# A hybrid attention layer on one core: keys loaded into the place of their lo, and fourteen steps of gate sets before them

## The chip, the cores and the metric

The kernel runs on one core of a Trainium2 chip (trn2). The metric is device time in microseconds (us) of one execution of the whole program; lower is better. The granted clock of TensorE is read from the profile; its two levels are 1.2 and 2.4 GHz.

## What is computed

One decoder layer on 1024 tokens of width 1024, all in float32: a SwiGLU feed-forward block, then a mixer, then a second SwiGLU block and a final norm. Each block has an RMS norm whose scale and shift come from a condition vector. Only the mixer matters here:

```python
u = modulate(rmsnorm(h, norm2_w), sh2, sc2)
proj = u @ w_in            # q, six key/value sets, gates, retention q k v g, ga, gb
o_nsa = nsa_attention(...) # compressed, selected and sliding-window branches, 8 heads, 2 key groups
o_ret = retention(...)     # 8 heads, chunks of 128 tokens, a state carried from chunk to chunk
mixed = sigmoid(ga) * (o_nsa @ w_nsa_up) + sigmoid(gb) * (o_ret @ w_ret_up)
h = h + gt2 * (mixed @ w_out)
```

Products keep float32 accuracy on TensorE by splitting each operand into a rounded part ("hi") and the rest ("lo") and taking three products, hi x hi, hi x lo and lo x hi.

## The kernel before

**Engines.** TensorE multiplies; ScalarE makes the hi parts (a copy that rounds), VectorE the lo parts (a subtraction); GpSimd does sums; all loads and stores of this part are issued on SP, one queue, in order. The program is written with generators; `weave(main, fill, n)` takes a step of `main` and after it `n` steps of `fill`. The framework's scheduler then orders the instructions of each engine, and each engine runs its own in that order.

**Gate sets.** The projection is computed in sets by a scheme of seven products for two blocks of 128 columns (`set_t` with `wset` and `seven`). A set loads two raw weight blocks of 512 KB (L327) into two of the three places of the tile `raw` (the pool `W2`, `WM = (3, 3)`: three places of `wp` and three of `raw`). GpSimd forms sums of them (L341 to L344, tile `S`), ScalarE and VectorE split them into `wp` (L334, L335). Each product is 12 matmuls of 128x512 (L281), in the order u0, u0, t2, t3, t4, u1, u1 by the name of its moving operand; the results are added up (L391 to L416). The first two products need only the first raw block, the third needs the sums of both. Eight such sets (0 to 7) make the gates `ga` and `gb`: their results pass a sigmoid (L1461) and are stored to `d_gab` (L1462). One set before them makes the keys, which are stored to `d_k` in memory, and two make the queries (`d_q`).

**Retention.** `ret_core` runs twice, once for four heads each, over eight chunks. A chunk is a chain across the engines: load q and k (L903) into `rqk`, rotate (L910 on VectorE, L912 and L913 on GpSimd), transpose (L918), scores (L928), mask (L930), output and state (L937 to L952), mean (L956 to L959), squares and variance (L961, L964). After every fourth chunk the outputs are scaled (L970, L975), gated (L977, with `rg` loaded at L974), transposed (L979), copied to `rb` (L982) and stored to `d_ret` (L983). Steps of the sets are the fill between the chunks' steps.

**Keys and queries.** After the retention a pool `kv` is opened where the retention's pool was; it holds Kh and Kl, hi and lo of two kinds of keys, 128 x 2 x 1024 each, and Q. `keys` loads four halves from `d_k`, each with two loads (L1027) that put the same data on partitions 0 to 63 and 64 to 127, and splits each (L1029, L1030). The halves pass through `self.stage()`, a place of `raw`. `queries` does the same with Q (L1055 to L1057). Then attention begins; its first score products (L1071 with Kh, L1072 with Kl) read Q and the keys, into the four places of `s`.

The part of `run` that sets the order before the change:

```python
        for _ in range(7):
            next(fill, None)
        kv = pool(c_n, "kv", "right")
        self.Q = {}
        weave(itertools.chain(self.keys(kv), self.queries(0, kv, self.stage)), fill, 3)
        drain(fill)
```

The fill holds 77 steps of sets beside the second retention's own; the compression and the two retentions take 40 of them, so that 7, 18 and 12 are left for these three statements.

Of the kernel before, what the change touches and what calls it, by code (L numbers as in the profile page):

```python
# [33 lines left out]
def drain(*gens):  # L34
    for g in gens:
        for _ in g:
            pass


def weave(main, fill, n):  # L40

    done = 0
    for i, _ in enumerate(main, 1):
        while done < i * n:
            next(fill, None)
            done += 1


def f32(ap):
    return ap.bitcast(F32)  # L50


class Layer:
# [963 lines left out]
    def keys(self, pool):  # L1017
        nc = self.nc
        self.Kh = [pool.tile([P, 2, T], F32R, name="Kh%d" % b) for b in range(2)]
        self.Kl = [pool.tile([P, 2, T], F32R, name="Kl%d" % b) for b in range(2)]  # L1020
        for b in range(2):
            src = self.d_k[b].rearrange("(g d) t -> d g t", g=2)
            for hf in range(2):
                s = slice(hf * H2, (hf + 1) * H2)
                a = self.stage()
                for r in range(2):
                    nc.sync.dma_start(a[64 * r:64 * r + 64], src[:, :, s])  # L1027
                kh, kl = self.Kh[b][:, :, s], self.Kl[b][:, :, s]
                nc.scalar.copy(kh, a)  # L1029
                nc.vector.tensor_sub(kl, a, f32(kh))  # L1030
                yield

    def values(self, pool, stage):
# [262 lines left out]
    def run(self):  # L1296
# [3 lines left out]
        nc = self.nc  # L1300
        self.w_in = self.I["w_in"][0].rearrange("(k p) n -> p k n", p=P)

        def pool(ctx, name, side="left"):
            return ctx.enter_context(tc.tile_pool(name=name, bufs=1, side=side, reuse_waits="tile"))
# [178 lines left out]
        def sets():  # L1483
            yield from self.set_t(self.w_in, 768, 1024, us, sp, to({"a": self.d_k[0], "b": self.d_k[1]}))
            for p in (0, 2):
                yield from self.set_t(self.w_in, p * P, (p + 1) * P, us, sp, to({"a": self.d_q[p], "b": self.d_q[p + 1]}))
            for d in range(KD):
                yield from self.set_t(self.w_in, 3352 + d * P, 4376 + d * P, us, sp, to_gate(d))
# [3 lines left out]
        fill = itertools.chain(more, sets())  # L1492
        with ExitStack() as c1:
            weave(self.compress(self.keep, pool(c1, "cmp", "right")), fill, 4)
        for r in range(2):
            with ExitStack() as c1:
                weave(self.ret_core(r, pool(c1, "ret", "right")), fill, 1)
            drain(more)
        for _ in range(7):
            next(fill, None)  # L1500
        kv = pool(c_n, "kv", "right")
        self.Q = {}
        weave(itertools.chain(self.keys(kv), self.queries(0, kv, self.stage)), fill, 3)
        drain(fill)


# [88 lines left out]
```

## Time and profile before

| | us |
|---|---|
| median of 3 runs (2422.99 to 2425.41) | 2424.69 |
| the profiled execution | 2428.69 |
| its span, first to last instruction | 2427.0 |
| PE busy in the span | 2271.1 (94%) |
| DVE busy (VectorE) | 1811.0 (75%) |
| POOL busy (GpSimd) | 1222.3 (50%) |
| ACT busy (ScalarE) | 1051.5 (43%) |

The mean granted clock of TensorE is 0.969 of full speed. In the rows, PE is a matmul, PEld its weight load, SPq a DMA issue on SP; times are from the start of the span. A row of a timeline gives start, duration, engine, line, operation, out<-in, count, and in brackets the idle time before it and what ended that. TensorE's matmuls overlap a little, so that the time of many is read from start to start.

### The profile page before, as it was taken

To read this page: it belongs to the slowest core of one execution; us is meant where nothing else is said; L and a number is where in the kernel's file an instruction comes from. 1 tells how busy PE (TensorE), PEld (TensorE's weight loads), DVE (VectorE), ACT (ScalarE), POOL (GpSimd) and SP (SyncE) were. 2 spreads that over 40 slices of the span, in tenths; PEclk is the share of its full clock that TensorE was granted. 3 is DMA by queue.
4 is the path that set the end of the run, shared out by engine and by line. 5 is a ranking of instruction groups with operands and counts; after the bars stand their busy time and mean duration, and the time that the engine had idled before them with its cause. 6 is when DMAs were issued, how large, how long until landed. Compare 5 with 4: busy or idle time off the path is not lost. (4 is left out here: it accounts for less than half of the span.)

```text
span 2427.0 us, 32641 instructions
## 1 busy us (share of the span) xinstructions
PE 2271.1 (94%) x11563; PEld 1903.5 (78%) x11563; DVE 1811.0 (75%) x2742; ACT 1051.5 (43%) x1902; POOL 1222.3 (50%) x900
## 2 busy tenths in 40 slices
PE   7799999999987999999869999999889999999997
PEld 5678888878876899887757889877668888887885
DVE  8888888578999844667646888859895555558988
ACT  5332222235764322223336777826532222235675
POOL 3856454544476524454434544645664444436437
PEclk8999999999998999999979999989899999999999
DMA  9135656263204444335343311470312222246301
GB/s 348 57 105 168 205 171 202 87 230 131 87 1 146 121 124 129 120 95 159 98 122 129 96 58 44 160 227 1 104 56 83 87 79 79 83 144 220 98 28 70
DMA packets 248886, 288.31 MB, mean 119 GB/s; under 512 B 14852, under 2 KB 169236, under 8 KB 248724
## 3 DMA queue, kind: packets, MB, share of 16 engines
q1 hardware_dynamic: 248608, 286.19, 37.1%
q8 instruction: 91, 1.49, 0.3%
q14 instruction: 71, 0.58, 0.1%
q10 hardware_dynamic: 116, 0.05, 0.0%
HBM read 216.45 MB, written 69.73 MB: 118 GB/s over the span
## 5 line engine op out<-in xcount | busy, mean ns | idle before, releaser
L281 PE MATMUL po<-u0h,wp 128*128 128x512 f32 x944 | 308.2, 399 | 24.1 <-ACT wp L334 14.6
L758 PE MATMUL po<-wp 128*128 128x512 f32 x1128 | 271.7, 398 | 15.6 <-DVE wp L679 14.7
L281 PE MATMUL po<-u1h,wp 128*128 128x512 f32 x880 | 283.2, 392 | 2.5 <-DVE bias L544 2.2
L758 PEld LDWEIGHTS po<-wp 128*128 128x128 f32 x1128 | 214.6, 192 | 68.4 <-DVE wp L679 22.2
L758 PE MATMUL s<-wp 128*128 128x512 f32 x1056 | 250.8, 394 | 13.9 <-DVE wp L679 13.3
L758 PEld LDWEIGHTS s<-wp 128*128 128x128 f32 x1056 | 199.7, 190 | 60.5 <-DVE wp L679 18.2
L334 ACT CAST wp<-S 128x1024 fp32r<-128x1024 f32 x98 | 103.0, 1051 | 299.8 <-PE po L281 295.7
L281 PEld LDWEIGHTS po<-u0h,wp 128*128 128x128 f32 x944 | 181.7, 192 | 64.4 <-ACT wp L334 15.0
L463 POOL TENSOR_TENSOR t<-t,t 128x512 f32<-128x512 f32 x38 | 56.3, 1482 | 297.9 <-DVE t L407 189.2
L281 PEld LDWEIGHTS po<-u1h,wp 128*128 128x128 f32 x880 | 165.9, 189 | 39.1 <-DVE bias L544 2.6
L281 PE MATMUL po<-u0l,wp 128*128 128x512 f32 x472 | 187.8, 398 | 0.0
L281 PE MATMUL po<-u1l,wp 128*128 128x512 f32 x440 | 172.9, 393 | 2.5 <-DVE u1l L243 2.5
L335 DVE TENSOR_TENSOR wp<-S,wp 128x1024 fp32r<-128x1024 f32 x98 | 158.7, 1620 | 15.3 <-ACT wp L334 15.2
L334 ACT CAST wp<-raw 128x1024 fp32r<-128x1024 f32 x98 | 82.0, 837 | 173.7 <-PE po L281 168.7
L341 POOL TENSOR_TENSOR S<-raw 128x512 f32<-128x512 f32 x49 | 68.4, 1396 | 141.1 <-DMA raw<-w_in 77.9
L281 PE MATMUL po<-t4h,wp 128*128 128x512 f32 x392 | 131.8, 397 | 1.8 <-DVE tn L399 1.1
L281 PE MATMUL po<-t3h,wp 128*128 128x512 f32 x392 | 131.8, 396 | 0.8 <-DVE t L395 0.8
L281 PE MATMUL po<-t2h,wp 128*128 128x512 f32 x392 | 131.3, 395 | 0.3 <-DVE tg L412 0.3
L335 DVE TENSOR_TENSOR wp<-raw,wp 128x1024 fp32r<-128x1024 f32 x98 | 114.9, 1173 | 13.7 <-ACT wp L334 13.5
L395 DVE TENSOR_TENSOR t<-tn,po 128x512 f32<-128x512 f32 x57 | 39.1, 685 | 101.2 <-issue 73.7
L1164 DVE TENSOR_TENSOR pl<-pt,ph 128x512 fp32r<-128x512 f32 (+2 forms) x160 | 96.8, 619 | 15.6 <-ACT ph L1163 15.0
L281 PEld LDWEIGHTS po<-u0l,wp 128*128 128x128 f32 x472 | 91.2, 193 | 18.9
(474 smaller groups left out, 6187.2 us busy)
## 6 DMA issues: line engine op xcount, KB each, us to landing
raw<-ffn_w_in SPq DMA_DIRECT2D x88, 512.0 KB, 4.2
raw<-ada_w SPq DMA_DIRECT2D x56, 512.0 KB, 4.4
raw<-w_in SPq DMA_DIRECT2D x40, 512.0 KB, 4.3
d_g<-t SPq DMA_DIRECT2D x50, 256.0 KB, 2.0
d_h<-hT SPq DMA_DIRECT2D x24, 512.0 KB, 4.7
hT<-d_h SPq DMA_DIRECT2D x48, 256.0 KB, 5.4
d_g<-tg SPq DMA_DIRECT2D x38, 256.0 KB, 2.0
fw<-ada_w SPq DMA_DIRECT2D x8, 1024.0 KB, 11.7
```

The costliest lines, as they stand in the source:

```text
L281: nc.tensor.matmul(ps, a, b, start=k == 0 and q == 0, stop=k == n - 1 and q == 2)
L334: nc.scalar.copy(w[:, 0], t)
L335: nc.vector.tensor_sub(w[:, 1], t, f32(w[:, 0]))
L341: nc.gpsimd.tensor_add(s[:, 0:4], b[:, 0:4], b[:, 4:8])
L395: nc.vector.tensor_add(c, u2, p)
L463: nc.gpsimd.tensor_mul(g, g, t)
L758: nc.tensor.matmul(po[d], l[:, e], r, start=k == 0 and z == 0 and not seeded, stop=k == m - 1 and z == 2, skip_group_check=seeded)
L1164: nc.vector.tensor_sub(lo, pt[:, :n], f32(hi))
```

## The change

Each half of the keys is loaded straight into its place in Kl, seen as float32; ScalarE rounds it from there into Kh, and VectorE subtracts Kh from it in place. The keys use no place of `raw` any more; the queries still do. Before the pool of the keys is opened, 14 steps of the fill are taken in place of 7, that is, two sets, and beside keys and queries 2 a step in place of 3 (12 in place of 18); 11 are left for the last statement. Everything computed is the same. Behind L1026 the line numbers of the changed kernel are lower by one.

```diff
@@ keys
             for hf in range(2):
                 s = slice(hf * H2, (hf + 1) * H2)
-                a = self.stage()
+                kh, kl = self.Kh[b][:, :, s], self.Kl[b][:, :, s]
                 for r in range(2):
-                    nc.sync.dma_start(a[64 * r:64 * r + 64], src[:, :, s])
-                kh, kl = self.Kh[b][:, :, s], self.Kl[b][:, :, s]
-                nc.scalar.copy(kh, a)
-                nc.vector.tensor_sub(kl, a, f32(kh))
+                    nc.sync.dma_start(f32(kl[64 * r:64 * r + 64]), src[:, :, s])
+                nc.scalar.copy(kh, f32(kl))
+                nc.vector.tensor_sub(kl, f32(kl), f32(kh))
                 yield
@@ run
-        for _ in range(7):
+        for _ in range(14):
             next(fill, None)
         kv = pool(c_n, "kv", "right")
         self.Q = {}
-        weave(itertools.chain(self.keys(kv), self.queries(0, kv, self.stage)), fill, 3)
+        weave(itertools.chain(self.keys(kv), self.queries(0, kv, self.stage)), fill, 2)
         drain(fill)
```

How the order moves, at three places. First SP, from the last loads of the retention (L974) on; L983 stores the retention's output, the loads from `d_k` and `d_q` are keys and queries, L327 are weights of a set, and the stores to `d_gab` are gates. Before:

```order
L974 DMA rg<-d_rn 128x256 x2
L983 DMA d_ret<-rb 128x512 x2
L1027 DMA raw<-d_k 64x2x512 x2
L327 DMA raw<-w_in 128x8x128 x2
L1055 DMA raw<-d_q 64x2x512 x4
L327 DMA raw<-w_in 128x8x128 x2
L1462 DMA d_gab<-t_10108 128x512
L327 DMA raw<-w_in 128x8x128
L1462 DMA d_gab<-t_10160 128x512
L327 DMA raw<-w_in 128x8x128
```

And now:

```order
L974 DMA rg<-d_rn 128x256 x2
L1461 DMA d_gab<-t_10248 128x512
L327 DMA raw<-w_in 128x8x128
L983 DMA d_ret<-rb 128x512 x2
L1027 DMA Kl_10003<-d_k 64x2x512 x4
L1027 DMA Kl_10004<-d_k 64x2x512 x4
L1461 DMA d_gab<-t_10294 128x512
L1461 DMA d_gab<-tg 128x512
L1461 DMA d_gab<-tn 128x512
L327 DMA raw<-w_in 128x8x128
```

All eight key loads now stand together behind the retention's last store, where six of them stood earlier; of the six weight loads that stood behind the retention, one stands ahead of its last store and one behind the keys, the other four earlier still. The two weight loads left are those of gate set 7.

Second, TensorE at the end of the retention's last chunk (L937 and L939 make its output, L979 transposes the gated outputs). Before:

```order
L928 MATMUL pi<-qT,kT 128x128 x4
L937 MATMUL po<-state_8761,qT 128x128
L939 MATMUL po<-rv,inn 128x64 x2
L937 MATMUL po<-state_8761,qT 128x128
L939 MATMUL po<-rv,inn 128x64 x2
L979 MATMUL po<-ident,xc 128x128 x8
L281 MATMUL po<-u0h,wp 128x512
L281 MATMUL po<-u0l,wp 128x512
```

And now:

```order
L937 MATMUL po<-state_8761,qT 128x128
L939 MATMUL po<-rv,inn 128x64 x2
L937 MATMUL po<-state_8761,qT 128x128
L939 MATMUL po<-rv,inn 128x64 x2
L281 MATMUL po<-u1h,wp 128x512
L281 MATMUL po<-u1l,wp 128x512
L281 MATMUL po<-u1h,wp 128x512 x2
L281 MATMUL po<-u1l,wp 128x512
```

Between the last chunk's output and the transposes there are now a whole product of set 5 (u1) and three of set 6; the first group of transposes stands ahead of set 6's fourth product (t3), the second behind eight of its twelve matmuls. The eight score products of the first attention tile stand, as before, behind a set's second product, now that of gate set 7 (one of the eight a product earlier).

Third, VectorE some 50 us earlier, between two gate sets (L410 to L416 add up the older set's last products, L335 splits the next set's weights, L910 rotates a chunk of the retention). Before:

```order
L407 TENSOR_TENSOR t_9861<-tg,po 128x512
L335 TENSOR_TENSOR wp<-raw,wp 128x1024
L910 TENSOR_TENSOR rb<-rqk,rcs 128x8x32 x2
L411 TENSOR_TENSOR tn<-tn,po 128x512
L412 TENSOR_TENSOR tg<-tg,po 128x512
```

And now:

```order
L407 TENSOR_TENSOR t_9861<-tg,po 128x512
L335 TENSOR_TENSOR wp<-raw,wp 128x1024
L411 TENSOR_TENSOR tn<-tn,po 128x512
L412 TENSOR_TENSOR tg<-tg,po 128x512
L335 TENSOR_TENSOR wp<-S,wp 128x1024
```

The rotation has moved behind the two additions that free the older set's results (and behind a split and the next addition).

## Rows read from the trace of the kernel before

**Rows 1.** The page's first part: busy time, share of the span, instructions.
```profile
PE 2271.1 (94%) x11563; PEld 1903.5 (78%) x11563; DVE 1811.0 (75%) x2742; ACT 1051.5 (43%) x1902; POOL 1222.3 (50%) x900
```
**Rows 2.** Busy time by stretches: PE, PEld, DVE, ACT, POOL, PEclk, DMA share, GB/s.
```profile
1050.00:1100.00 50.00, 49.57 (x278) 41.05 (x277) 34.71 (x63) 13.84 (x19) 20.48 (x20) 1.00 0.33 101
1100.00:1150.00 50.00, 48.01 (x282) 39.06 (x280) 34.64 (x61) 14.06 (x22) 28.07 (x25) 1.00 0.51 154
...
1200.00:1250.00 50.00, 27.28 (x141) 21.57 (x140) 25.62 (x45) 16.86 (x21) 10.57 (x12) 0.69 0.40 108
```
**Rows 3.** Timeline of PE, from the retention's last chunk to the first scores.
```profile
1209.50 0.46 PE L937 MATMUL po<-state,qT 128*128 128x128 f32 x2 [2.22 <-DVE xc L959]
...
1216.49 1.35 PE L979 MATMUL po<-ident,xc 128*128 128x128 f32 x4 [4.65 <-DVE xc L977]
1219.12 1.37 PE L979 MATMUL po<-ident,xc 128*128 128x128 f32 x4 [1.27 <-DVE xc L977]
1235.07 0.79 PE L281 MATMUL po<-u0h,wp 128*128 128x512 f32 x1 [14.58 <-ACT wp L334]
...
1243.29 0.39 PE L1071 MATMUL s<-Kh,Q 128*128 128x512 f32 x1
...
1244.78 0.40 PE L281 MATMUL po<-t2h,wp 128*128 128x512 f32 x1
```
**Rows 4.** Timeline of PE: the starts of u0 and of t2, two products apart.
```profile
1152.95 0.39 PE L281 MATMUL po<-u0h,wp 128*128 128x512 f32 x1
...
1158.39 0.39 PE L281 MATMUL po<-t2h,wp 128*128 128x512 f32 x1
```
**Rows 5.** Timeline of SP: issues of keys and of weights.
```profile
1136.77 0.59 SPq L1027 DMA_DIRECT2D raw<-d_k  x1
...
1162.23 0.48 SPq L327 DMA_DIRECT2D raw<-w_in  x1
...
1188.37 0.59 SPq L1027 DMA_DIRECT2D raw<-d_k  x1
...
1227.28 1.24 SPq L1027 DMA_DIRECT2D raw<-d_k  x2
1228.61 1.33 SPq L327 DMA_DIRECT2D raw<-w_in  x2
```
**Rows 6.** Timeline of ACT: casts of keys and of weights, and a sigmoid.
```profile
1223.74 2.94 ACT L1029 CAST Kh<-raw 128x1024 fp32r<-128x1024 f32 x3
1232.40 1.04 ACT L1029 CAST Kh<-raw 128x1024 fp32r<-128x1024 f32 x1 [5.73 <-DMA raw<-d_k]
1233.97 1.04 ACT L334 CAST wp<-raw 128x1024 fp32r<-128x1024 f32 x1 [0.53 <-DMA raw<-w_in]
...
1249.48 0.63 ACT L1461 ACTIVATE t<-t 128x512 f32<-128x512 f32 x1
```
**Rows 7.** Timeline of PE: the second product of a wait further up, first and next.
```profile
1175.31 0.47 PE L281 MATMUL po<-u0h,wp 128*128 128x512 f32 x1 [2.18 <-DVE tg L412]
...
1179.73 0.60 PE L918 MATMUL pt<-ident,rqk 128*128 128x128 f32 x4
```
**Rows 8.** Timeline of DVE: a rotation, the keys' lo, the sets' last addition.
```profile
1171.04 2.93 DVE L910 TENSOR_TENSOR rb<-rqk,rcs 128x256 f32<-128x256 f32 x2
...
1226.03 3.50 DVE L1030 TENSOR_TENSOR Kl<-raw,Kh 128x1024 fp32r<-128x1024 f32 x3 [6.28 <-DMA d_ret<-rb]
...
1296.84 0.69 DVE L416 TENSOR_TENSOR tn<-tn,po 128x512 f32<-128x512 f32 x1 [1.44 <-PE po L281]
```
**Rows 9.** Timeline of POOL: the first and the third sum of gate set 5.
```profile
1235.75 1.66 POOL L341 TENSOR_TENSOR S<-raw 128x512 f32<-128x512 f32 x1 [18.17 <-DMA raw<-w_in]
...
1238.61 1.28 POOL L342 TENSOR_TENSOR S<-S,raw 128x512 f32<-128x512 f32 x1
```
**Rows 10.** The view of line L1027, the eight key loads of 256 KB.
```profile
DMA to landing us min/median/max: 3.6/3.9/5.6
```
**Rows 11.** The view of line L327, the weight loads of 512 KB.
```profile
DMA to landing us min/median/max: 3.8/4.2/8.8
```

## The prediction

> **What bounds the kernel now.** I read the page's first part, then the busy time by stretches, then TensorE's timeline in the worst stretch, and from its longest wait back through the queues. TensorE (PE) is busy 94% of the span [rows 1], so only stretches where it stands still can give much. One such lies in the middle: from 1050 to 1150 us it idles 0.4 and 2.0 us per 50, from 1200 to 1250 it is busy 27.3 us and its granted clock averages 0.69 [rows 2]. That is the end of the retention, just before the keys. The timeline names four waits there: 2.22 us (VectorE's centred output), 4.65 and 1.27 (its gated output), 14.58 (ScalarE's cast of the next gate set's weights); together 22.7 [rows 3]. From the first of them until after the last the matmuls run slow: the 24 of gate set 5's first two products take from 1235.07 to 1243.29, 8.2 us [rows 3], where 24 like them take from 1152.95 to 1158.39, 5.44, or 2.72 for a product of 12 [rows 4].
>
> Why were those weights so late? Sets take their raw weights from three `raw` places, and the key halves take the same three. The first key load is issued at 1136.8, the sixth at 1188.4, and no weights are issued between 1162.23 and 1228.61 [rows 5]. The keys cannot leave their places: their hi and lo lie where the retention's tiles lie, so the first cast is at 1223.74 [rows 6]. From about 1190 on, the retention's latency has nothing beside it.
>
> **The change, part by part.** The two edits belong together: loading the keys into Kl takes them off `raw`, and 14 steps in place of 7 lets sets be planned ahead of the keys.
>
> *Taken away.* (1) In the new order nearly eleven products of gate sets 5 and 6 (11 x 2.72 = 30 us) move ahead of the last retention transposes, so the four waits have work in them: **22.7 us**. (2) TensorE does not slow there: 8.2 - 5.4 = 2.8 us on the 24 matmuls, and half of the 2.7 us of the two transpose groups [rows 3], 1.3; together **4.1**. (3) Earlier, matmuls start again at 1175.31 after waiting 2.18 us for VectorE's L412 and run slow, 12 of them until 1179.73: 4.4 in place of 2.7 [rows 7]. L412 stood behind the rotary products L910, which took 2.93 us [rows 8]; in the new order L411 and L412 stand ahead of L910. **3.9 us**; it may also stay. Sum 30.7.
>
> *Moved.* The eight key loads no longer run early. Kl's place overlaps the retention's `rb`, so the first load waits until the second store of d_ret has landed. Call E the end of the last transposes (before: 1219.12 + 1.37 = 1220.5 [rows 3]). VectorE waited for that store until 1226.03 [rows 8], E + 5.5. From there I take the flow of the trace of before: a pair of key loads issued at 1227.28, then two weights loads from 1228.61 [rows 5]; the pair was cast at 1232.40, the first weights at 1233.97 [rows 6], and GpSimd took the second at 1235.75 [rows 9]. So the first half MB lands 5.1 us after its issue, each further one 1.6 to 1.8 later; I take 1.7. The four pairs then land at E + 10.6, 12.3, 14.0 and 15.7. SP issues the eight in 8 x 0.62 = 5.0 us (two in 1.24 [rows 5]), done at E + 10.5; the stores behind them wait for results that come later anyway. Each pair is cast in 1.05 us [rows 6] and subtracted in about 1.2 (three in 3.50 [rows 8]). The same instructions were there before, on the same sizes; that they now read and write one tile I cost at nothing.
>
> Who waits? TensorE has, after E, a third of a product and five whole ones (5.33 x 2.72 = 14.5 us), then the eight score products of the first attention tile, about 1.5 us (1243.29 [rows 3] to the next L281 at 1244.78 [rows 3]), so they could end at E + 16.0. Those on the window keys need all four pairs: 15.7 + 1.05 + 1.2 = 17.9, and end near 18.4.
>
> Behind them stands the third product of gate set 7, which needs sums of both its weight loads. The second of these is now on SP behind the eight key loads and three stores of set 6, the last of which waits for a sigmoid that stands on ScalarE behind the second key cast: 12.3 + 1.05 + 0.63 [rows 6] = 14.0. Issued at 14.4, it lands at 18.6 by the median of 4.2 for half a MB [rows 11], or behind the keys at 17.4; I take 18.6. Then GpSimd's three sums, 4.1 us (1235.75 to 1239.9 [rows 9]), cast and subtraction, 2.3: ready at E + 25.0. So **9.0 us** of new waiting (25.0 - 16.0), of which 2.4 is the keys' and 6.6 the weights'. After it I take the slow start that followed the old wait, **2.8**. And **1.5** for ordinary pace beside the retention, between the 0.4 and 2.0 idle per 50 us of [rows 2]; GpSimd now has set 5's four sums among the retention's rotary work there, which is the likeliest part of it. Together 13.3.
>
> Bounds of the new wait: below, 0, if loads run faster than the queue shows; above, each pair takes as long as a single load's median, 3.9 [rows 10], in place of 1.7: the last pair lands at 22.3, the weights at 26.2, ready 32.6, wait 16.6. I take 9.0, since the rows of three half MBs in a row are the nearest.
>
> *At nothing.* Masks and values for attention need places that set 7 frees; their loads were issued 10 us and more before use and still follow the sums, ahead of 13.6 us of products. If that cover failed it would cost one load, 4 us.
>
> **The sum.** 30.7 - 13.3 = 17.4 us. Against the profiled execution, 2428.69 - 17.4 = 2411.3; that execution lies 4.0 above the median of the runs, so the median goes from 2424.69 to **2407.3**. About 0.2% (5 us) is what the measurement can tell from no change.
>
> The Trainium skill speaks against this change: "Trainium Kernel Development and Optimization", section Best Practices, asks to overlap loads with compute by double buffering, and here an early load is made late. The trace of before shows the overlapped load being the one that does the harm [rows 5]; by the rule alone the sum would be only the 9 us added, and its case is the last rival.
>
> **The rivals.**
> - *All hidden* (0.12): the loads are done before TensorE comes to them, and no slow start follows. 30.7 - 1.5 = 29.2 gained, 2395.5. Against it: SP's new order, in which the weights stand behind the keys.
> - *The wait mostly moves* (0.18): pairs land 3.9 apart, wait 16.6. 30.7 - 16.6 - 2.8 - 1.5 = 9.8 gained, 2414.9; without term (3), 5.9 and 2418.8. For it: a single key load of a quarter MB does take 3.9 to land [rows 10]. Against: the three half MBs in [rows 5, 6, 9].
> - *No change to speak of* (0.06): the same, with the order of the first attention tiles, which also shifts, costing a few us.
> - *Slower* (0.04): the exposed keys become the bound. If each of the eight loads waited for the one before (8 x 3.9), the last would land at E + 36.7, the weights at 40.9, ready at 47.2: wait 31.2, and 30.7 - 31.2 - 2.8 - 1.5 is 4.8 lost, 2429.5. It decides from about 7.1 us between pairs, since then the new wait of 26.4 eats the gain; the trace shows a quarter of that.
>
> That the change does nothing of the kind is ruled out by the new order itself.
>
> **The numbers.** The forecast case (gain 12 to 23) has 0.60. The range 2397 to 2417 leaves out the best part of the first rival, the worst of the second, and the last two. Faster: 0.60 + 0.12 + 0.18 = 0.90; same 0.06; slower 0.04.
>
> **What would show it.** Right: no weights gap of 66 us on SP; no wait over 3 us on TensorE before the last L979; sets' end (1296.84 before, the last L416 [rows 8]) about 17 us earlier; one wait of some 6 us for ScalarE or VectorE's split of S at gate set 7's third product, just after the eight scores, and a shorter one for Kh or Kl before it. Wrong: the key loads landing over 3 us apart, a wait over 10 us there, or the gain lost again between the first scores and the end of attention.

## The result, and the profile after

| | before | after |
|---|---|---|
| median of 4 runs each, us | 2425.05 (2422.99 to 2427.16) | 2411.85 (2408.05 to 2412.32) |
| the profiled execution, us | 2428.69 | 2412.32 |
| its span, us, and mean granted clock | 2427.0, 0.969 | 2410.2, 0.976 |

The ratio is 0.9942, 95% interval 0.9925 to 0.9959: 13.2 us faster by the medians, 10 to 18 by the interval. The changed kernel ran again beside three experiments: 2410.89 us, ratio 0.9946 (0.9933 to 0.9960). The two profiled executions lie 16.4 apart.

Lines past L1026 are one lower in the kernel after. The whole is little changed in the page's first part ([rows 1] before):

```profile
PE 2265.5 (94%) x11563; PEld 1901.0 (79%) x11563; DVE 1814.0 (75%) x2742; ACT 1052.2 (44%) x1902; POOL 1218.8 (51%) x900
```

The busy time by stretches, columns as in [rows 2], shows where it went. The stretch from 1200 to 1250 us, busy 27.28 at a clock of 0.69 before, is full; a smaller hole stands one stretch later.

```profile
1050.00:1100.00 50.00, 49.54 (x260) 40.94 (x259) 35.16 (x63) 14.36 (x20) 20.38 (x20) 1.00 0.36 112
1100.00:1150.00 50.00, 48.00 (x282) 39.02 (x281) 35.30 (x65) 12.96 (x20) 27.84 (x26) 1.00 0.50 148
1150.00:1200.00 50.00, 48.50 (x245) 39.86 (x244) 32.80 (x47) 19.85 (x27) 29.18 (x24) 1.00 0.41 127
1200.00:1250.00 50.00, 49.56 (x258) 40.27 (x256) 32.08 (x57) 20.26 (x28) 11.01 (x14) 1.00 0.44 119
1250.00:1300.00 50.00, 34.59 (x149) 26.25 (x149) 31.31 (x83) 27.10 (x52) 24.02 (x21) 0.90 0.46 145
```

TensorE's timeline there, against [rows 3]: the last transposes (L979) come without a wait, E is 1233.48 + 0.60 = 1234.08, and behind them stand waits for the keys' hi (2.42) and lo (0.70) and for set 7's third product (6.20), 9.3 us in all.

```profile
1231.18 0.60 PE L979 MATMUL po<-ident,xc 128*128 128x128 f32 x4
...
1233.48 0.60 PE L979 MATMUL po<-ident,xc 128*128 128x128 f32 x4
...
1252.38 0.56 PE L1070 MATMUL s<-Kh,Q 128*128 128x384 f32 x2 [2.42 <-ACT Kh L1028]
1253.64 0.56 PE L1071 MATMUL s<-Kl,Q 128*128 128x384 f32 x2 [0.70 <-DVE Kl L1029]
1260.40 0.80 PE L281 MATMUL po<-t2h,wp 128*128 128x512 f32 x1 [6.20 <-ACT wp L334]
...
1265.87 0.40 PE L281 MATMUL po<-t3h,wp 128*128 128x512 f32 x1
```

SyncE's queue gives the reason for the longest, as [rows 5] did for the old one: the eight key loads stand behind the second store of d_ret, and set 7's second weights behind them, issued at E + 15.0.

```profile
1234.72 3.05 SPq L983 DMA_DIRECT2D d_ret<-rb  x2
1239.56 5.17 SPq L1027 DMA_DIRECT2D Kl<-d_k  x8
...
1249.06 0.39 SPq L327 DMA_DIRECT2D raw<-w_in  x1
```

ScalarE casts the first key pair at 1244.73 as soon as it has landed, the fourth at 1251.28, and set 7's sum of weights at 1259.31, after a wait for GpSimd (its timeline; before: [rows 6]):

```profile
1244.73 1.05 ACT L1028 CAST Kh<-Kl 128x1024 fp32r<-128x1024 f32 x1 [3.46 <-DMA Kl<-d_k]
...
1251.28 1.05 ACT L1028 CAST Kh<-Kl 128x1024 fp32r<-128x1024 f32 x1 [0.39 <-DMA Kl<-d_k]
...
1259.31 1.04 ACT L334 CAST wp<-S 128x1024 fp32r<-128x1024 f32 x1 [4.46 <-POOL S L342]
```

GpSimd in turn waited for those weights (its timeline; before: [rows 9]); they landed 6.5 us after their issue:

```profile
1255.58 1.26 POOL L341 TENSOR_TENSOR S<-raw 128x512 f32<-128x512 f32 x1 [26.04 <-DMA raw<-w_in]
```

The sets' last addition on VectorE comes at 1276.99 in place of 1296.84 ([rows 8]), 19.85 us earlier:

```profile
1276.99 0.69 DVE L416 TENSOR_TENSOR tn<-tn,po 128x512 f32<-128x512 f32 x1 [1.44 <-PE po L281]
```

Not all of that is the change's. The retention's first store of d_ret, far ahead of anything the change moves, came 2.90 us earlier in this execution. Up to the first key load (1136.77 us before, [rows 5]) every engine issues the same instructions in the same order in both kernels, so this is run to run; just ahead of that load the distance is 3.1 us. Here is the store in SyncE's timeline, first of the kernel before, then of the kernel after:

```profile
1023.45 0.32 SPq L983 DMA_DIRECT2D d_ret<-rb  x1
```

```profile
1020.55 0.32 SPq L983 DMA_DIRECT2D d_ret<-rb  x1
```

19.85 - 2.90 leaves **16.95 us** gained between there and the sets' end. Some of it is given back in attention: the last value product of its first part starts at 1583.38 before and at 1565.97 after, 17.4 us earlier in place of 19.85, so 2.4 were lost. These are two rows of TensorE's timeline, of the kernel before and of the kernel after:

```profile
1583.38 0.41 PE L1174 MATMUL ot<-pl,t2h 128*128 128x256 f32 x1
```

```profile
1565.97 0.28 PE L1173 MATMUL ot<-pl,t2h 128*128 128x256 f32 x1
```

So 16.95 - 2.4 = 14.5 are left of the gain there, against 13.2 by the medians; the profiled pair's 16.4 flatters the change.

### The profile page after: what moved, and what is told of

Its sections match the earlier page's. It is cut to its first block, busy times and chain, and to the rows that moved or that the text cites. A ratio compares the mean times of both kernels' runs of the same rounds, so it can differ in the third digit from the quotient of the medians.

```text
span 2410.2 us, 32648 instructions
## 1 busy us (share of the span) xinstructions
PE 2265.5 (94%) x11563; PEld 1901.0 (79%) x11563; DVE 1814.0 (75%) x2742; ACT 1052.2 (44%) x1902; POOL 1218.8 (51%) x900
## 4 chain that ended last, share of the span: by engine, by line
PE 37%; DVE 10%; DMA 4%; issue 2%; ACT 2%; POOL 1%; SPq 0%; DVEq 0%; ACTq 0%; POOLq 0%
PE po L281 21%; DVE wp L679 3%; PE po L758 3%; PE s L758 3%; PE ot L1173 2%; PE pt L1159 2%; PE s L281 1%; PE s L1071 1%; PE po L495 1%; PE s L1070 1%; DVE hT L789 1%; DVE wp L335 1%; DMA rqk<-d_rn 1%; PE ot L1170 0%; DMA t4h<-d_on 0%
## 5 line engine op out<-in xcount | busy, mean ns | idle before, releaser
L335 DVE TENSOR_TENSOR wp<-S,wp 128x1024 fp32r<-128x1024 f32 x98 | 160.0, 1632 | 21.2 <-ACT wp L334 21.0
L335 DVE TENSOR_TENSOR wp<-raw,wp 128x1024 fp32r<-128x1024 f32 x98 | 114.5, 1168 | 12.4 <-ACT wp L334 12.2
L281 PEld LDWEIGHTS po<-u0l,wp 128*128 128x128 f32 x472 | 89.7, 190 | 18.4
```

The source lines that it names most:

```text
L281: nc.tensor.matmul(ps, a, b, start=k == 0 and q == 0, stop=k == n - 1 and q == 2)
L335: nc.vector.tensor_sub(w[:, 1], t, f32(w[:, 0]))
```

## Experiments

The theory: the gain needs two things at once, `raw` places that the keys no longer hold, and gate sets that stand in the program ahead of the keys; and what is left of the hole is set 7's second weights, late because the queries still hold two of the three `raw` places. Four groups of runs test it. The reference is 2424.0 to 2424.5 us for the kernel before on each chip, and 2410.9 to 2411.9 for the whole change; where a run did not have the whole change beside it on its chip, it is the ratios to the kernel before that compare. What some expectations call a decay load or store is read here as the retention's store of d_ret (L983).

**1. Either half of the change alone.** The place alone, with the old steps (edit against the whole change):

```diff
-        for _ in range(14):
+        for _ in range(7):
-        weave(itertools.chain(self.keys(kv), self.queries(0, kv, self.stage)), fill, 2)
+        weave(itertools.chain(self.keys(kv), self.queries(0, kv, self.stage)), fill, 3)
```

> The new place of the keys alone: they are loaded into the lo place and split there, but the retention's end again takes seven steps ahead of the keys and three with each step of them, as in the kernel before. The reference points are 2425.1 us for the kernel before and 2411.9 us with the whole change. Theory A (the places free the weight loads, and the steps taken ahead decide which gate set stands beside the last two chunks of the retention): the gate sets stand as in the kernel before, so the half-clock stretch and the 14.6 us wait are gone only in part. The key loads stand on SP behind the last decay load and set 6's last and set 7's first weights behind them, so the third product of set 6 waits some 6 to 10 us for its weights: 2413 to 2421 us. Rival R1 (the place does it, since the order of the program's steps is made up for by the scheduler): 2411 to 2413 us. Rival R2 (the steps do it alone): 2424 to 2426 us, no change.

Measured: 2425.3 us, ratio to the kernel before 1.0004 (0.9995 to 1.0013). No change, and 4 us above what the theory expected; the number is the one that the second rival gave, and the next run decides against that rival. Its timeline of TensorE shows that the waits in the retention's tail are gone, and that most of the waiting has moved behind it, 18.4 us in these three rows: with seven steps there are products enough for the transposes, but none are left to cover the keys. The theory had one wait of 6 to 10 us for weights; the longest is for the keys.

```profile
1245.59 0.79 PE L1070 MATMUL s<-Kh,Q 128*128 128x512 f32 x1 [12.15 <-ACT Kh L1028]
...
1252.47 0.90 PE L1070 MATMUL s<-Kh,Q 128*128 128x384 f32 x2 [2.53 <-ACT Kh L1028]
...
1258.37 0.79 PE L281 MATMUL po<-t2h,wp 128*128 128x512 f32 x1 [3.74 <-ACT wp L334]
```

The steps alone, with the keys staged as before (edit against the whole change):

```diff
-                kh, kl = self.Kh[b][:, :, s], self.Kl[b][:, :, s]
+                a = self.stage()
...
-                    nc.sync.dma_start(f32(kl[64 * r:64 * r + 64]), src[:, :, s])
-                nc.scalar.copy(kh, f32(kl))
-                nc.vector.tensor_sub(kl, f32(kl), f32(kh))
+                    nc.sync.dma_start(a[64 * r:64 * r + 64], src[:, :, s])
+                kh, kl = self.Kh[b][:, :, s], self.Kl[b][:, :, s]
+                nc.scalar.copy(kh, a)
+                nc.vector.tensor_sub(kl, a, f32(kh))
```

> The steps alone: fourteen are taken ahead of the keys and two with each step of them, but the keys are staged in two raw places as in the kernel before. Theory A: with the raw places held by the staged keys and queries, the weights of the last sets cannot be loaded beside the retention's tail; the products of the early sets move ahead of the tail and chunks 6 and 7 stand with little beside them, so the waits of 2.2 to 4.7 us on DVE come back, and the wait for weights behind the keys with them: 2422 to 2432 us. Rival R1 (the place does it all): 2424 to 2426 us, as the kernel before. Rival R2 (the steps do it alone): 2411 to 2413 us.

Measured: 2429.72 us, ratio 1.0029 (1.0020 to 1.0037), slower, as the theory expected. Here is its timeline of TensorE: the old waits on VectorE and a 15.46 us wait for weights, at set 6's third product where [rows 3] have it at set 5's first.

```profile
1207.93 0.76 PE L937 MATMUL po<-state,qT 128*128 128x128 f32 x2 [2.22 <-DVE xc L959]
...
1215.37 1.35 PE L979 MATMUL po<-ident,xc 128*128 128x128 f32 x4 [4.65 <-DVE xc L977]
...
1235.35 0.80 PE L281 MATMUL po<-t2h,wp 128*128 128x512 f32 x1 [15.46 <-ACT wp L334]
```

Neither half gives a microsecond; together they give 13. Both rivals fall.

**2. Why the rest of the hole stays: the place of Kl, or the queries.** First the memory: lo places allocated ahead of hi places, which is meant to let no key load land in memory that a tile of the retention still uses.

```diff
-        self.Kh = [pool.tile([P, 2, T], F32R, name="Kh%d" % b) for b in range(2)]
...
+        self.Kh = [pool.tile([P, 2, T], F32R, name="Kh%d" % b) for b in range(2)]
```

> The whole change with the lo places of the keys allocated ahead of the hi places, so that no key load lands in memory that a tile of the retention still uses; the first key load need not wait for the landing of the last decay load. Theory A (of the 9.3 us that TensorE still waits there, 6.2 us are set 7's second weights, which stand on SP behind eight key loads and three stores): the keys come some 2 to 3 us earlier, the waits of 2.4 and 0.7 us at the transposes go, the weights come earlier by as much, if their place in SP's order is what sets them: 2407 to 2410 us, 2 to 5 us below the whole change. Rival R3 (the place that set 7's weights land in is held by the queries until they are split, and sets them): the waits at the keys go and come back at the weights: 2411 to 2413 us. Rival R4 (the keys are late because the transfers themselves are slow, 2 us a pair): 2411 to 2413 us, with the waits at the keys unchanged.

Measured: 2410.5 us, ratio 0.9945 (0.9931 to 0.9958): not told apart from the whole change. The loads do come sooner: the first is issued 0.37 us behind the issue of the second store of d_ret (1238.69 and 1238.32), where it stood 2.10 behind (1239.56 and 1237.46). In its timeline of TensorE the three waits shrink by 1.0, 0 and 0.55 us.

```profile
1252.01 0.56 PE L1070 MATMUL s<-Kh,Q 128*128 128x384 f32 x2 [1.38 <-ACT Kh L1028]
1253.27 0.55 PE L1071 MATMUL s<-Kl,Q 128*128 128x384 f32 x2 [0.70 <-DVE Kl L1029]
1259.48 0.79 PE L281 MATMUL po<-t2h,wp 128*128 128x512 f32 x1 [5.65 <-ACT wp L334]
```

Then more steps ahead of the keys, but fewer than it takes to bring set 7 ahead of the queries:

```diff
-        for _ in range(14):
+        for _ in range(21):
-        weave(itertools.chain(self.keys(kv), self.queries(0, kv, self.stage)), fill, 2)
+        weave(itertools.chain(self.keys(kv), self.queries(0, kv, self.stage)), fill, 1)
```

> The whole change with twenty-one steps ahead of the keys and one with each step of keys and queries, in place of fourteen and two. Theory A (the last set's second weights stand in the program behind the queries as long as fewer than 31 steps are taken ahead, so nothing that waits is moved): as the whole change, 2408 to 2413 us, with a wait of 5 to 7 us for weights at set 7's third product. Rival R1 (each further step ahead of the keys helps): 2400 to 2407 us.

Measured: 2411.14 us, ratio 0.9943 (0.9930 to 0.9955), as the whole change, with the wait where it was (timeline of TensorE):

```profile
1261.01 0.80 PE L281 MATMUL po<-t2h,wp 128*128 128x512 f32 x1 [5.82 <-ACT wp L334]
```

Then the queries after the last gate set:

```diff
-        weave(itertools.chain(self.keys(kv), self.queries(0, kv, self.stage)), fill, 2)
+        weave(self.keys(kv), fill, 2)
         drain(fill)
+        drain(self.queries(0, kv, self.stage))
```

> The whole change with the queries loaded after the last gate set instead of ahead of its end: the two raw places are then free for set 7's second weights, which are loaded ahead of the last decay load. Theory A: the 6.2 us wait for weights goes, and the slow start of 2.8 us behind it; the scores stand among set 7's products, so the keys' waits of 3.1 us are covered too. 9 to 12 us less than the whole change: 2400 to 2405 us. Rival R4 (the attention's first tiles wait for queries that now come last): the wait moves to the first attention scores, which need the split queries, 2409 to 2413 us, with a wait of 4 us or more for Q there. Rival R5 (the wait is not the weights but VectorE, behind on the sets' tails): same as the whole change, 2411 to 2413 us.

Measured: 2407.1 us, ratio 0.9929 (0.9916 to 0.9941), some 4 us below the whole change, where 9 to 12 were expected. The wait for weights is gone; where the rest of what was expected went is not shown (in its profile the way from the first store of d_ret to the sets' end is 7.1 us shorter, 249.30 against 256.44). Its SyncE timeline has the last weights 20 us ahead of the last stores of d_ret:

```profile
1221.50 0.38 SPq L327 DMA_DIRECT2D raw<-w_in  x1
...
1241.35 0.33 SPq L983 DMA_DIRECT2D d_ret<-rb  x1
```

What TensorE then waits for is short: the keys, and VectorE's tail of a set (its timeline):

```profile
1257.30 0.49 PE L1071 MATMUL s<-Kl,Q 128*128 128x512 f32 x1 [0.77 <-DVE Kl L1029]
...
1269.34 0.50 PE L281 MATMUL po<-u1h,wp 128*128 128x512 f32 x1 [1.51 <-DVE t L407]
```

**3. A fourth `raw` place.** If places are the cause, one more should do it without touching the order of the program:

```diff
-WF, WM = (4, 4), (3, 3)
+WF, WM = (4, 4), (3, 4)
```

> The whole change, and a fourth raw place in the mixer's weight pool; nothing else is edited. Reference points: 2425 us the kernel before, 2411.9 us the whole change, 2407.1 us the change with the queries loaded last. Theory A (set 7's second weights came late since the two queries held two of the three raw places until VectorE and ScalarE split them): with a fourth place these weights stand on SP ahead of the last decay stores, the 6.2 us wait at the third product of set 7 goes, the scores are spread among the products and the keys' waits of 3.1 us shrink under 2 us: 2404 to 2408 us. Rival R1 (it is the program's order, the queries ahead of the set, and not the count of places): the wait stays, 2411 to 2413 us. Rival R2 (the key loads themselves are the limit): the wait moves to the scores and stays 6 us or more, 2410 to 2413 us.

Measured: 2397.08 us, ratio 0.9889 (0.9875 to 0.9902), 13.8 us below the whole change on the same chip, and 7 better than the theory's best. That repeat of the whole change was run with it:

> The whole change unaltered, on the same chip as the three others: 2408 to 2413 us, and the first attention scores 112 to 118 us behind the first transposes of chunk 6, as in its first profile; a shift of the whole program of up to 3 us before those transposes is run to run.

It took 2410.89 us. Read from the output transposes (L979) that start at 1161.47 to the first scores behind the sets, at 1278.76, the distance is 117.3 us, as expected. From the first store of d_ret to the sets' end it took 256.16 us, 256.44 in the first profile. With the fourth place TensorE has one wait over half a microsecond left between the last transposes and the sets' end, 3.49 us for the keys (timeline of TensorE):

```profile
1242.42 0.50 PE L1070 MATMUL s<-Kh,Q 128*128 128x512 f32 x1 [3.49 <-ACT Kh L1028]
```

The part beyond the theory's best lies further up and further down. In the same run's stretches TensorE is busy 49.59 us from 1100 to 1150 where the whole change has 48.00; and the clock from 1250 to 1300 stays at 1.00, where it was 0.90.

```profile
1050.00:1100.00 50.00, 50.00 (x263) 41.36 (x262) 34.63 (x61) 14.96 (x21) 22.35 (x24) 1.00 0.38 117
1100.00:1150.00 50.00, 49.59 (x292) 41.25 (x291) 35.07 (x68) 15.03 (x23) 28.26 (x25) 1.00 0.49 148
...
1200.00:1250.00 50.00, 46.51 (x222) 38.00 (x221) 34.80 (x51) 23.02 (x30) 12.09 (x13) 0.97 0.50 139
1250.00:1300.00 50.00, 46.04 (x259) 38.65 (x259) 35.71 (x106) 32.62 (x64) 25.96 (x24) 1.00 0.42 138
```

Why the earlier stretch is fuller is not shown: the waits that shrank there stood on VectorE (0.76 and 1.07 us in the whole change, none and 0.41 here), not on weights, and with the fourth place the order of the instructions differs from some 755 us on.

Is a spare place all that the kernel before lacked? The same edit on the kernel before:

> The kernel before with a fourth raw place and nothing else: keys staged in raw places, seven steps ahead of the keys and three with each of them. Theory A (places and planned sets are needed together: with seven steps ahead there is no further set in the program that the spare place could feed beside the last two chunks): the waits on DVE in the retention's tail and the long wait for weights behind it stay; only the 2 to 3 us that the fourth place gave back ahead of chunk 6 come: 2420 to 2425 us. Rival R1 (a spare place is all that was missing): 2397 to 2412 us.

Measured: 2422.03 us, ratio 0.9989 (0.9981 to 0.9998): 2.5 us, as expected. Its timeline of TensorE keeps the old waits, of which the longest is still 11.85 us; the theory's reason is that no further set stands ahead of the keys:

```profile
1208.85 1.35 PE L979 MATMUL po<-ident,xc 128*128 128x128 f32 x4 [4.65 <-DVE xc L977]
...
1224.73 0.79 PE L281 MATMUL po<-u0h,wp 128*128 128x512 f32 x1 [11.85 <-ACT wp L334]
```

And with the steps of the change but staged keys (the second edit of group 1 and the fourth place):

> The steps of the change (fourteen ahead, two with each step of the keys) with the keys staged in raw places as in the kernel before, but with a fourth raw place. Reference points: 2429.7 us the same with three places, 2411.9 us the whole change. Theory A (places are what the change gains: two staged keys and two staged queries leave one of three places for weights, and it takes two to feed a set): with a fourth place the products stand beside the tail of the retention again and the waits of 2.2 and 4.7 us on DVE go; the scores stand right behind the last transposes and wait there for keys, and set 7's weights still come behind: 2412 to 2420 us, more than half of the change's gain over the 2429.7 us. Rival R1 (the direct load of the keys, not the count of places, makes the gain): 2424 to 2430 us.

Measured: 2417.13 us, ratio 0.9973 (0.9963 to 0.9982): 12.6 of the 18 us between the steps alone and the whole change come back without the direct load. The times alone do not show that the direct load works through the places it frees: a fourth place is worth as much with it (13.8 us), and with four places the direct load is still worth 20.0 (2417.13 against 2397.08). The queue shows it. In this run the staged keys fill all four places, and SyncE issues no weights from 1174.54 to 1232.33 (its timeline):

```profile
1174.54 0.38 SPq L327 DMA_DIRECT2D raw<-w_in  x1
...
1203.29 1.25 SPq L1027 DMA_DIRECT2D raw<-d_k  x2
...
1231.01 1.24 SPq L1055 DMA_DIRECT2D raw<-d_q  x2
1232.33 1.33 SPq L327 DMA_DIRECT2D raw<-w_in  x2
```

What TensorE then waits for are the queries, 14.58 us, which get their places only when the keys have left theirs (its timeline):

```profile
1238.86 0.80 PE L1071 MATMUL s<-Kh,Q 128*128 128x512 f32 x1 [14.58 <-DVE Q L1057]
```

**4. All of it.** The whole change with the fourth place and the lo places first (the edits of groups 3 and 2):

> The whole change with the fourth raw place, and the lo places of the keys allocated ahead of the hi places. With the fourth place alone (2397.1 us) what is left behind the last transposes is a wait of 3.5 us for the first hi tile of the keys. Theory A (the first key load waits there for the landing of the last decay store, whose tile lies where the lo place is put): the key loads come 1.5 to 2.5 us earlier and the wait falls under 2 us: 2394 to 2397 us. Rival R1 (only the transfers' pace of some 2 us a pair counts): no change, 2396.5 to 2398 us.

Measured: 2396.51 us, ratio 0.9878 (0.9863 to 0.9893). The first key load comes 1.8 us earlier behind the transposes, as expected, but the wait falls only from 3.49 to 2.13 (timeline of TensorE), and the time, which both expectations allow, is not told apart from 2397.08.

```profile
1241.84 0.79 PE L1070 MATMUL s<-Kh,Q 128*128 128x512 f32 x1 [2.13 <-ACT Kh L1028]
```

With the queries last as well:

> Three edits on the whole change together: the lo places of the keys allocated ahead of the hi places, the queries loaded after the gate sets, and a fourth raw place. Theory A: no weights are late, the keys come some 1.5 us earlier, and the scores among set 7's products wait under 1 us: 2402 to 2407 us, at or a little below the best so far. Rival (what is left there is VectorE's, the tails of the gate sets and the split of the queries): as the queries last, 2406 to 2408 us.

Measured: 2396.14 us, ratio 0.9884 (0.9871 to 0.9898). Better than expected, and the same as the fourth place alone: once the weights are early, neither the queries' order nor the keys' memory is worth a microsecond that these runs can show. Three versions near 2396.5 beat both kernels; the simplest is the one number of group 3.

## Why the prediction came out right

It forecast 2407.3 us and a gain of 17.4; the medians give 2411.85 and 13.2.

- **Taken away.** The longest time without weights on SyncE there is 28.6 us (1203.83 to 1232.39) in place of 66. Terms (1) and (2) held: no wait of TensorE from 1185 us to E is over 0.6 us, and the clock there is 1.00. Of term (3) the wait for L412 went, but one of 1.25 us (at 1183.05, for another step of a set's tail) stands near it; the prediction had said that it might stay.
- **The new wait.** Forecast 9.0, of which 2.4 the keys' and 6.6 the weights'; measured 3.1 and 6.2, together 9.3, at the places named. The first pair was cast at E + 10.65 (forecast 10.6). That these sums came so close is in part luck: two steps were short and one was long. The last pair was cast at 1251.28, E + 17.2 (forecast 15.7), since pairs came 1.9 to 2.3 apart and not 1.7. And the weights took 6.5 us to land, not 4.2: issued at E + 15.0 (forecast 14.4), ready at E + 26.3 (forecast 25.0). From their landing the forecast took 6.4 us for three sums, cast and subtraction; measured are 4.8 (1255.58 to 1260.40), since the product's first matmul starts when the cast is done (1259.31 + 1.04, and 1260.40) and does not wait for the subtraction, as 1233.97 + 1.04 and 1235.07 in [rows 6] and [rows 3] had already shown. And the scores, held by the keys, ended at E + 20.1 and not E + 18.4, so that less of the lateness was left to wait for.
- **Slow start.** Forecast 2.8; the 12 matmuls from 1260.40 to 1265.87 take 5.47 in place of 2.72 [rows 4], 2.75 more.
- **Pace.** Forecast 1.5; between 1150 and 1250 TensorE idles 1.50 + 0.44 = 1.9 us, of which 1.25 are the wait just named.
- **The sum at the sets' end.** 17.4 forecast, 16.95 measured once the 2.90 us that lie ahead of the change are taken off.
- **What failed** is the end: the prediction carried the gain unchanged to the end of the program, and named a loss in attention only as a sign of being wrong. Attention took 1565.97 - 1276.99 = 289.0 us in place of 286.5; in the repeat it was 288.5. In most experiments it lies at 287.4 to 288.8, with the fourth place alone at 286.2, with all edits together at 291.6. Its instructions stand in another order than in the kernel before. But the steps alone and the fourth place, whose traces have one and the same order of attention on TensorE, VectorE, ScalarE and GpSimd, took 288.8 and 286.2, so the order alone does not set the length; and there is one profile of the kernel before to compare with. Whether the change costs attention anything stays open.

Of the rivals, "all hidden" did not come (2395.5 was forecast for it; the fourth place, which hides the weights and gains further up too, comes to 2397.1). Something like "the wait mostly moves" came in one half of the change, the place alone, where 18.4 us of waiting stand behind the tail. "Slower" came in the other half, by another mechanism: the steps without the places. The rule that the Trainium skill gives ("Trainium Kernel Development and Optimization", Best Practices: overlap transfers with compute by double buffering) does not speak against this change as the forecast let it: an early load that has nowhere to go but a place others need is no overlap. Where the buffer was added for the loads that feed TensorE, the runs agree with the rule, by 13.8 us on top of the whole change and by 2.5 on the kernel before.

## What to carry to other kernels

A prefetch that cannot leave its staging buffer is a lock on everything that shares the buffer: look in the queue for a gap in the *other* users' loads (66 us here), not at the wait itself. Taking the holder out gains only if the program has work ready to enter the freed places, and ordering that work early gains only if there are places; try the two edits together, and price a spare buffer along with them: here one number was worth as much again on top of the whole change, and 2.5 us on the kernel before. When comparing two profiles, look first at a landmark ahead of the change: here it already differed by 2.9 us of the 16.8 between the two spans.

## What the runs showed of the hardware that was not expected

Key loads in a row took longer each, from their own issue to their landing. A key load of 256 KB took 3.9 us by its median before [rows 10]; the same eight, issued without a pause, take 5.9 in the kernel after (view of line L1027):

```profile
DMA to landing us min/median/max: 5.5/5.9/7.0
```

The pairs still came 1.9 to 2.3 us apart, and the half MB of weights issued 4.3 us behind the end of the last key load's issue took 6.5 against a median of 4.2 [rows 11]. The row is not shown to be the only cause: staged keys, not in a row, took 5.2 by the median in the kernel before with a fourth place. And the more TensorE had waited, the lower its mean granted clock was in these stretches of 50 us: with waits adding to 22.7 us the stretch from 1200 to 1250 had 0.69 [rows 2]; with 9.3 the stretch from 1250 to 1300 of the whole change had 0.90, and with 2.75 and 5.76 in the repeat 0.86; with one of 3.49 in it, the fourth place's stretch from 1200 to 1250 had 0.97. The two profiles of one kernel show that this is no strict measure.
